# Neighbourhood attention with rows' and context's scores in one two-bank tile, and an output projection that begins with the first pair of heads

## The chip, the core and the metric

The kernel runs on one core of a Trainium2 chip. The metric is the time of one execution on the device, in microseconds (us); smaller is better. Profiles come from one execution each, recorded by the hardware profiler; the engines are TensorE (PE, with its weight loads as PEld), VectorE (DVE), ScalarE (ACT), GpSimd (POOL) and SyncE (SP), which issues the DMAs.

## What is computed

One layer of a diffusion backbone on 1024 latent tokens (16 rows of 64) and 256 context tokens, width 1024. Cut to what matters here:

```python
o_na = neighborhood_attention(q, k, v, k_ctx, v_ctx, rpb)     # 8 heads of 64
o_g, _ = bidirectional_gdn(...)                               # 4 heads of 128, two directions
y = concat([o_na * silu(na_z), o_g * silu(g_z)]) @ w_out
x = x + gate * rmsnorm(y, g_post)
```

Each query of the attention sees a window of 8 rows by 16 columns of latent keys, with a learned bias for each row and column offset, and all 256 context keys, in one softmax:

```python
s_loc = q_r . k_win + bias          # 128 window scores
s_ctx = q_r . k_ctx                 # 256 context scores
p = softmax(concat([s_loc, s_ctx]))
out = p_loc . v_win + p_ctx . v_ctx
```

The gated delta scan runs forwards and backwards over chunks, each step from the state of the one before.

## The kernel before, in words

Phases 0 to 2 (to about 555 us) project the inputs, convolve, and prepare the scan's chunk matrices. This part of the program is the same in both kernels. `phase_b` is the mixed stage: `na_attn` (line 597) and `delta_scan` (line 1170) are generators that yield between pieces of work, and `phase_b` (lines 1460 to 1463) takes pieces of the scan in a fixed proportion to those of the attention. The matmuls of both are chained in the order in which they are written (`pe`, line 592), so PE runs them in that order; the other engines' queues are ordered by the scheduler of the tile framework, and a tile's buffer is given to its next user when all readers of the whole tile are done.

The attention works on 32 units: 4 pairs of heads, 2 halves of the rows (rt), 4 blocks of columns (ct). A unit has two half-units, one for each head of the pair, numbered i. For a half-unit:

- `na_scores` (line 716). POOL adds bias and mask (gm, line 729; not for ct = 2, which takes that of ct = 1). PE makes 256 context scores into the tile pc (line 736) and 288 or 384 window scores into pl (line 739), two matmuls each, since a query is split in a high and a low part. DVE reduces pc to its negated maximum mi (line 744); a second DVE pass over pl and gm writes the negated biased scores and, starting from mi, the negated maximum nm (line 745). ACT takes the exponential of the rows' scores from SBUF (line 746), then that of the context's scores from pc (line 747), each with its own sum.
- `na_turn` (line 751), one iteration later: PE transposes the context's two blocks back into pc (line 754), ACT copies them out (tcx, line 756), PE transposes the rows' three blocks into pl (line 758), DVE copies them out (tl, line 760).
- `na_values` (line 763): matmuls of the values (lines 769 and 774), for both halves of a unit at once, into po.

pc and pl have two buffers each, of one PSUM bank. At the end of a half of the rows, `values` and `end` divide by the sums and multiply by the gate (lines 622 to 639); a finished pair goes to the DRAM buffer m_dram, the last pair is split straight into a high and a low part for the projection (`split_m`, line 704).

A scan step (`delta_step`, line 1194) has three phases for PE (lines 1210, 1228 and 1239, two directions each, two instructions per direction), with POOL (kd line 1204, vb line 1208), DVE (y line 1212, the new state line 1242) and ACT (vn lines 1231 and 1233) between them, and two products for the output (lines 1217 and 1250).

`phase4` (line 1301) multiplies m, in eight blocks k of 128 channels, by w_out: three matmuls of 512 columns for each block and output tile (lines 1337 to 1339). Seven of the first eight output tiles are accumulated block by block in the order `W_ORDER`; block 3, the last pair, comes first. The weights are split into high and low parts in pieces of 512 columns, each loaded to one of two buffers, copied by ACT and subtracted by POOL (`split_piece`, line 693); four blocks and one high part are split early, in buffers that the attention and the scan have given up (`w_out_early`, line 672).

Of the kernel before, what the change touches and what calls it, by code (L numbers as in the profile page):

```python
# [11 lines left out]
F32 = mybir.dt.float32  # L12
# [8 lines left out]
P = 128  # L21
# [115 lines left out]
W_ORDER = [3, 0, 1, 2, 4, 5, 6, 7]  # L137


class K:  # L140
# [456 lines left out]
    def na_attn(self, na, ps):  # L597
# [11 lines left out]

        pairs = {0: load(0)}  # L610
# [4 lines left out]
        def values(j):  # L615
# [17 lines left out]
        def end(j):  # L633
# [12 lines left out]
            if p == 2:  # L646
                self.wait_w = 6
                self.w_out_early(self.pf, [("qh0", 8), ("ql0", 8), ("qh1", 8), ("ql1", 8), ("kk0", 10), ("kk1", 10)])

        for i in range(2 * len(units) + 3):  # L650
            if i < 2 * len(units):
                j, hh = divmod(i, 2)
                p, rt, ct = units[j]
                if (ct, hh) == (0, 0):
                    sums[p, rt] = self.nw.tile([P, 4, 2, 2], F32, name=f"sums{p}_{rt}", tag="sums", bufs=2)
# [12 lines left out]
            self.split_piece()  # L668
# [3 lines left out]
    def w_out_early(self, pool, tags):  # L672
        for tag, n in tags:
            w = pool.tile([P, n, P], F32, name=f"wo_{tag}{len(self.wos)}", tag=tag, bufs=1 if pool is self.pf else 2).rearrange(
                "p t c -> p (t c)")
            for o in range(0, n * P - D + 1, D):
                self.wos.append(w[:, o:o + D])
                if len(self.wos) % 2 == 0:
                    self.split_w(W_ORDER[len(self.wos) // 2 - 1], *self.wos[-2:])

    def split_w(self, k, hi, lo):
        self.wo[k] = (hi.bitcast(F32R), lo.bitcast(F32R))
        self.pieces.extend((k, o, hi[:, o:o + 512], lo[:, o:o + 512]) for o in (0, 512))
        self.load_pieces()

    def load_pieces(self):
        while self.pieces and len(self.staged) < 2:
            k, o, hi, lo = self.pieces.pop(0)
            raw = self.g3.tile([P, 512], F32, name=f"wor{k}_{o}", tag="wor", bufs=2)
            self.load(raw, self.I["w_out"][k * P:(k + 1) * P, o:o + 512], self.na_last)  # L690
            self.staged.append((raw, hi, lo))

    def split_piece(self, n=1):
        nc = self.nc
        if self.wait_w:
            self.wait_w -= 1
            return
        for _ in range(min(n, len(self.staged) + len(self.pieces))):
            raw, hi, lo = self.staged.pop(0)
# [814 lines left out]
```

## Time and profile before

| | us |
|---|---|
| median of 3 runs | 890.77 |
| the three runs | 889.36, 890.77, 899.58 |
| the profiled execution | 898.68 |
| its span, first to last instruction | 896.9 |
| first scores matmul of the attention (line 736) | 555.6 |
| first matmul of the output projection (line 1337) | 797.7 |
| PE busy | 837.1 |
| DVE, ACT, POOL busy | 542.1, 416.9, 352.8 |

The profiled execution is 7.9 us above the median; sums are made against its own time. In the rows of the profile, a group stands with its count, its busy time, the mean of one instruction in ns, and behind the second bar the engine's idle time just before it with what ended that idle time. In the rows by stretch stand the stretch, its length, then busy time with the number of instructions for PE, PEld, DVE, ACT and POOL, the granted clock of PE (1.00 is full), the busy share of the DMA engines and GB/s. In the timeline stand start, length, engine, line and operation. In a chain of waits stand start, length and what ran.

### The profile page before, as it was taken

To read this page: it belongs to the slowest core of one execution; us is meant where nothing else is said; L and a number is where in the kernel's file an instruction comes from. 1 tells how busy PE (TensorE), PEld (TensorE's weight loads), DVE (VectorE), ACT (ScalarE), POOL (GpSimd) and SP (SyncE) were. 2 spreads that over 40 slices of the span, in tenths; PEclk is the share of its full clock that TensorE was granted. 3 is DMA by queue.
4 is the path that set the end of the run, shared out by engine and by line. 5 is a ranking of instruction groups with operands and counts; after the bars stand their busy time and mean duration, and the time that the engine had idled before them with its cause. 6 is when DMAs were issued, how large, how long until landed. Compare 5 with 4: busy or idle time off the path is not lost.

```text
span 896.9 us, 16578 instructions
## 1 busy us (share of the span) xinstructions
PE 837.1 (93%) x6082; PEld 704.4 (79%) x6082; DVE 542.1 (60%) x1179; ACT 416.9 (46%) x1165; POOL 352.8 (39%) x415
## 2 busy tenths in 40 slices
PE   6999999999999979898989997899899999989996
PEld 4678887888788858688877876788788888868885
DVE  3453454556536699779649433577677787781332
ACT  4253535745653554563143533556455555661210
POOL 1333221734453442345512112646546566643110
PEclk9899999999999999999998986799999999989999
DMA  9687442265365535743899857978829523251251
GB/s 339 248 284 253 131 127 85 83 217 169 106 200 174 151 100 176 196 107 93 299 259 253 214 189 288 347 169 217 301 77 294 160 80 133 71 193 66 96 183 51
DMA packets 95175, 160.97 MB, mean 179 GB/s; under 512 B 28581, under 2 KB 55542, under 8 KB 92918
## 3 DMA queue, kind: packets, MB, share of 16 engines
q1 hardware_dynamic: 87606, 146.25, 52.5%
q10 hardware_dynamic: 7488, 13.67, 4.9%
q8 instruction: 48, 0.79, 0.4%
q14 instruction: 33, 0.27, 0.1%
HBM read 110.82 MB, written 52.42 MB: 182 GB/s over the span
## 4 chain that ended last, share of the span: by engine, by line
PE 61%; DVE 19%; DMA 11%; ACT 3%; issue 3%; SPq 2%; POOL 1%; DVEq 0%; POOLq 0%; ACTq 0%
PE py L1337 3%; PE py L1339 3%; PE py L1338 3%; DVE tb L1063 3%; DVE vb L1066 3%; PE pz L461 2%; PE pz L465 2%; PE pz L466 2%; DMA pm_dram<-pm 2%; PE pl L739 2%; PE po L774 2%; PE po L769 2%; PE pa L1228 2%; PE pc L736 2%; DMA tm_dram<-tm 2%
## 5 line engine op out<-in xcount | busy, mean ns | idle before, releaser
L729 POOL TENSOR_TENSOR gm<-gt,mk 128x288 f32<-128x288 f32 (+1 forms) x48 | 46.3, 969 | 40.4 <-DVE nm L745 40.4
L1204 POOL TENSOR_SCALAR kd<-kt,kd 128x128 f32<-128x128 f32 x72 | 42.7, 604 | 28.0 <-PE pa L1239 27.9
L746 ACT ACTIVATE pt<-pt,nm 128x288 f32<-128x288 f32 (+1 forms) x64 | 36.7, 574 | 30.2 <-DVE nm L745 29.9
L760 DVE COPY tl<-pl 96x384 f32<-96x384 f32 (+1 forms) x64 | 35.3, 552 | 17.3 <-PE pl L758 16.4
L745 DVE CUSTOM_DVE_ANT_0 pt<-pl,gm,mi 128x288 f32<-128x288 f32 (+1 forms) x64 | 36.3, 567 | 11.0 <-POOL gm L729 4.7
L1005 ACT ACTIVATE em<-em,gc 128x128 f32<-128x128 f32 x80 | 25.6, 391 | 34.3 <-DMA em<-gc_dram 29.3
L465 PE MATMUL pz<-hl,wh_gz 128*128 128x512 f32 x96 | 39.9, 415 | 0.0
L466 PE MATMUL pz<-hh,wl_gz 128*128 128x512 f32 x96 | 39.5, 412 | 0.0
L461 PE MATMUL pz<-hh,wh_gz 128*128 128x512 f32 x96 | 39.4, 410 | 0.0
L474 PE MATMUL pv<-wh_nv,hh 128*128 128x264 f32 x128 | 35.7, 298 | 2.0 <-ACT hh L263 1.6
L1208 POOL TENSOR_SCALAR vb<-v,beta 128x128 f32<-128x128 f32 x40 | 24.2, 606 | 32.6 <-DVE y L1212 16.7
L475 PE MATMUL pv<-wh_nv,hl 128*128 128x264 f32 x128 | 36.9, 293 | 0.0
L476 PE MATMUL pv<-wl_nv,hh 128*128 128x264 f32 x128 | 35.9, 290 | 1.0 <-DVE wl_nv L447 1.0
L1391 ACT ACTIVATE finv<-py 128x512 f32<-128x512 f32 x16 | 9.6, 599 | 57.3 <-PE py L1339 39.1
L1063 DVE TENSOR_TENSOR tb<-ab,vb 120x31 f32<-120x31 f32 (+15 forms) x62 | 30.2, 487 | 9.9 <-DMA ab<-ab_dram 8.3
L872 DVE SCALAR_TENSOR_TENSOR acc_v<-xp_v,cols,acc_v 128x1282 f32<-128x1282 f32 x16 | 29.1, 1818 | 10.9 <-ACT acc_v L870 10.6
L1392 DVE TENSOR_TENSOR finv<-py,ggb 128x512 f32<-128x512 f32 x16 | 11.0, 690 | 40.6 <-ACT finv L1391 40.5
L744 DVE TENSOR_REDUCE mi<-pc 128x1 f32<-128x256 f32 x64 | 26.9, 420 | 12.4 <-PE pc L736 11.6
L1024 POOL TENSOR_SCALAR_AFFINE_SELECT qe<-qe 128x256 f32<-128x256 f32 x32 | 24.2, 759 | 24.7 <-DVE qe L1023 24.3
L758 PE MATMUL pl<-c,pt 128*96 128x128 f32 (+1 forms) x192 | 32.1, 277 | 0.0
L1020 DVE SCALAR_TENSOR_TENSOR pm<-pk,beta,em 128x128 f32<-128x128 f32 x80 | 23.6, 343 | 13.1 <-PE pk L1013 10.9
L872 DVE SCALAR_TENSOR_TENSOR acc_q<-xp_q,cols,acc_q 128x1024 f32<-128x1024 f32 x16 | 20.5, 1284 | 17.0 <-ACT acc_q L870 16.7
(433 smaller groups left out, 2907.5 us busy)
## 6 DMA issues: line engine op xcount, KB each, us to landing
wada<-in_w_ada SPq DMA_DIRECT2D x16, 512.0 KB, 6.9
em<-gc_dram SPq DMA_DIRECT2D x20, 256.0 KB, 4.1
pm_dram<-pm SPq DMA_DIRECT2D x20, 256.0 KB, 3.2
pmf<-pm_dram SPq DMA_DIRECT2D x8, 640.0 KB, 7.0
tm_dram<-tm SPq DMA_DIRECT2D x8, 640.0 KB, 7.5
kk<-qk_dram SPq DMA_DIRECT2D x16, 320.0 KB, 9.1
tm<-tm_dram SPq DMA_DIRECT2D x4, 1280.0 KB, 16.1
kq_dram<-kq SPq DMA_DIRECT2D x4, 1152.0 KB
```

The costliest lines, as they stand in the source:

```text
L461: r = nc.tensor.matmul(ps, wh, xh, start=(k == 0), stop=False)
L465: nc.tensor.matmul(ps, wh, xl, start=False, stop=False)
L466: nc.tensor.matmul(ps, wl, xh, start=False, stop=(k == KC - 1))
L474: nc.tensor.matmul(ps, xh, wh, start=(k == 0), stop=False)
L475: nc.tensor.matmul(ps, xl, wh, start=False, stop=False)
L476: nc.tensor.matmul(ps, xh, wl, start=False, stop=(k == KC - 1))
L729: nc.gpsimd.tensor_tensor(self.gm[hh][:, :n].rearrange("p (n c r) -> p n c r", c=nco, r=4), gv, self.mk[:, mo:mo + n].rearrange("p (n c r) ...
L745: nc.vector.tensor_tensor_reduce(pt[:, :n], pl[:, :n], gm[:, :n], -1.0, mi, ALU.add, ALU.min, nm)
L746: nc.scalar.activation(pt[:, :n], pt[:, :n], AF.Exp, bias=nm, scale=-1.0, accum_out=sums[:, ct, hh, 0:1])
L872: nc.vector.scalar_tensor_tensor(av, xp[:, s0 + tap:s0 + tap + 1282 - s0], wc(tap), av, ALU.mult, ALU.add)
L1063: nc.vector.tensor_tensor(t3, bc(ab[:, 0:m, m:m + 1], [r, m, n]), bc(vb[:, m:m + 1, m:], [r, m, n]), ALU.mult)
L1204: nc.gpsimd.tensor_scalar(kd[d], kt_[:, t, :], self.kd[:, h, d, t:t + 1], None, ALU.mult)
```

## The change

- **One tile for a half-unit's scores.** sc has two banks: the rows' scores end at column 512 (pl), the context's lie from 512 to 768 (pc). gm becomes one of three fixed tiles of 640 columns whose last 256 are set to zero once; the bias and mask end at column 384. One DVE pass over 544 or 640 columns takes the place of the reduce and the pass, one exponential with one sum that of the two; the sums tile loses a dimension, and with it one addition for each half of the rows.
- **The turn.** All five transposes are written first, then the two copies. tcx, tl and the scan's y have one buffer less.
- **The start.** The scan begins two yields later and then runs slightly denser; its first kd and vb are ordered behind the last gm that was written before them.
- **The projection.** Block 0 comes first and block 3 second. After pair 2 the weights of blocks 0 and 3 are split early, and m of block 0 is read back from m_dram and split with the same pieces (ACT and POOL); block 1's weights follow in the last head of the scan, and half of block 2's. Pieces are split one per half-unit, two half-units or more after their load. The two-bank tiles serve as two output tiles each.

The core of the diff:

```diff
-W_ORDER = [3, 0, 1, 2, 4, 5, 6, 7]
+W_ORDER = [0, 3, 1, 2, 4, 5, 6, 7]
...
+        self.gms, self.gmi = [self.nw.tile([P, 640], F32, name=f"gm{i}") for i in range(3)], 0
+        for g in self.gms:
+            nc.gpsimd.memset(g[:, 384:], 0.0)
...
-            v = sums[p, rt]
-            nc.vector.tensor_tensor(rs.rearrange("p (a b) -> p a b", a=4), v[:, :, :, 0], v[:, :, :, 1], ALU.add)
-            nc.vector.tensor_scalar(rs, rs, 2.0, None, ALU.mult)
+            nc.vector.tensor_scalar(rs, sums[p, rt].rearrange("p a b -> p (a b)"), 2.0, None, ALU.mult)
...
             if p == 2:
-                self.wait_w = 6
-                self.w_out_early(self.pf, [("qh0", 8), ("ql0", 8), ("qh1", 8), ("ql1", 8), ("kk0", 10), ("kk1", 10)])
+                self.clock += 4
+                w = [self.pf.tile([P, n], F32, name=f"early_{t}", tag=t)[:, :D]
+                     for t, n in (("qh0", S), ("ql0", S), ("qh1", S), ("ql1", S), ("kk0", S + CT), ("kk1", S + CT))]
+                self.split_w(W_ORDER[0], *w[:2])
+                self.split_w(W_ORDER[1], *w[2:4])
+                self.ms[0] = tuple(v.bitcast(F32R) for v in w[4:])
+                self.split_later(self.m_dram[0:P, :], *w[4:])
+                self.clock -= 4
...
-            self.split_piece()
+            self.split_piece(1, 2)
...
         if ct != 2:
-            self.gm[hh] = self.nw.tile([P, 384], F32, name=f"gm{p}_{u}_{hh}", tag="gm", bufs=3)
-            nc.gpsimd.tensor_tensor(self.gm[hh][:, :n].rearrange("p (n c r) -> p n c r", c=nco, r=4), gv,
+            self.gm[hh] = self.gms[self.gmi % 3]
+            self.gmi += 1
+            r = nc.gpsimd.tensor_tensor(self.gm[hh][:, 384 - n:384].rearrange("p (n c r) -> p n c r", c=nco, r=4), gv,
                                     self.mk[:, mo:mo + n].rearrange("p (n c r) -> p n c r", c=nco, r=4), ALU.add)
+            self.last_gm = r.ins.name
...
-        pc = ps.tile([P, 512], F32, name=f"pc{p}_{u}_{hh}", tag="sc", bufs=2)[:, :256]
-        pl = ps.tile([P, 512], F32, name=f"pl{p}_{u}_{hh}", tag="sl", bufs=2)
+        sc = ps.tile([P, 1024], F32, name=f"sc{p}_{u}_{hh}", tag="sc", bufs=2)
+        pl, pc = sc[:, :512], sc[:, 512:768]
...
-        nc.vector.tensor_reduce(mi, pc, AX.X, ALU.max, negate=True)
-        nc.vector.tensor_tensor_reduce(pt[:, :n], pl[:, :n], gm[:, :n], -1.0, mi, ALU.add, ALU.min, nm)
-        nc.scalar.activation(pt[:, :n], pt[:, :n], AF.Exp, bias=nm, scale=-1.0, accum_out=sums[:, ct, hh, 0:1])
-        self.last_exp = nc.scalar.activation(pt[:, 384:640], pc, AF.Exp, bias=nm,
-                                             accum_out=sums[:, ct, hh, 1:2]).ins.name
+        nc.vector.tensor_tensor_reduce(pt[:, 384 - n:], sc[:, 512 - n:768], gm[:, 384 - n:], -1.0, 3.0e38, ALU.add, ALU.min, nm)
+        self.last_exp = nc.scalar.activation(pt[:, 384 - n:], pt[:, 384 - n:], AF.Exp, bias=nm, scale=-1.0,
+                                             accum_out=sums[:, ct, hh:hh + 1]).ins.name
...
+        for rc in range(3):
+            self.pe(nc.tensor.transpose(pl[:m, (rc + 1) * P:(rc + 2) * P], pt[:, 384 + (rc - 3) * m:384 + (rc - 2) * m], self.ident))
+        tcx = self.nw.tile([P, 2, P], F32, name=f"tcx{nm}", tag="tcx", bufs=3)
         nc.scalar.copy(tcx.rearrange("p c q -> p (c q)"), pc)
...
+                    w = [g3.tile([P, n, P], F32, name=f"early_{t}", tag=t, bufs=2).rearrange("p t c -> p (t c)")
+                         for t, n in (("o", 8), ("tm", 20))]
+                    self.spare = w[1][:, D:2 * D]
+                    self.split_w(W_ORDER[2], w[0], w[1][:, :D])
...
+                if (h, i) == (0, 0):
+                    self.order(r, self.last_gm)
...
-        late[W_ORDER[4]] = (self.wos[8], tl("wl", W_ORDER[4]))
+        late[W_ORDER[3]] = (self.spare, tl("wl", W_ORDER[3]))
+        late[W_ORDER[4]] = (tl("wh", W_ORDER[4]), tl("wl", W_ORDER[4]))
...
-        tags = [tag for tag, n in banks.items() for _ in range(n)]
+        tags = ["sc", "sc", "sc", "sc", "po", "pa0", "pa1", "os"]
...
-                    while done < min(118, (i + 1) * 118 // 130):
+                    while done < min(118, 1 + max(0, i - 2) * 117 // 127):
```

How the instructions move, at three places. First POOL, at the start of the mixed stage (vb and kd are the scan's, gm the attention's). Before:

```order
L1208 TENSOR_SCALAR vb_1_1_5774<-v_5737,beta 128x128
L1208 TENSOR_SCALAR vb_1_0_5819<-v_5737,beta 128x128
L1208 TENSOR_SCALAR vb_1_9_5887<-v_5737,beta 128x128
L1204 TENSOR_SCALAR kd_0_0_5770<-kt_5738,kd 128x128
L1204 TENSOR_SCALAR kd_1_1_5772<-kt_5738,kd 128x128
L1204 TENSOR_SCALAR kd_0_1_5812<-kt_5738,kd 128x128
L729 TENSOR_TENSOR gm_0_0_5721<-gt_0_5284,mk 128x288
L729 TENSOR_TENSOR gm_0_1_5751<-gt_1_5286,mk 128x288
```

Changed:

```order
L612 MEMSET gm_5718 128x256
L612 MEMSET gm_5719 128x256
L612 MEMSET gm_5720 128x256
L732 TENSOR_TENSOR gm_5718<-gt_0_5284,mk 128x288
L732 TENSOR_TENSOR gm_5719<-gt_1_5286,mk 128x288
L732 TENSOR_TENSOR gm_5720<-gt_0_5284,mk 128x384
L1209 TENSOR_SCALAR kd_0_0_5785<-kt_5739,kd 128x128
L1209 TENSOR_SCALAR kd_1_1_5787<-kt_5739,kd 128x128
L1215 TENSOR_SCALAR vb_1_1_5789<-v_5738,beta 128x128
```

The first three gm moved ahead of all of the scan's work on POOL.

Second DVE, in the last unit of the loop (a name's last numbers are unit and head; y, s and o are the scan's). Before:

```order
L744 TENSOR_REDUCE mi_7_0_8998<-pc_7_0_8992 128x1
L745 ISA pt_7_0_9000,nm_7_0_8999<-pl_7_0_8993,gm_7_0_8990,mi_7_0_8998 128x288
L745 ISA nm_7_0_8999 128x1
L760 COPY tl_6_1_9020<-pl_6_1_8927 128x384
L1242 SCALAR_TENSOR_TENSOR s_0_8_9025<-s_0_7_8950,egl,pa_0_8316 128x128
```

Changed:

```order
L748 ISA pt_7_0_8706,nm_7_0_8705<-sc_7_0_8700,gm_5719 128x544
L748 ISA nm_7_0_8705 128x1
L1251 SCALAR_TENSOR_TENSOR s_0_8_8727<-s_0_7_8663,egl,pa_0_8078 128x128
L1251 SCALAR_TENSOR_TENSOR s_1_3_8730<-s_1_4_8666,egl,pa_1_8079 128x128
L762 COPY tl_6_1_8724<-sc_6_1_8643 128x384
```

The reduce is gone, the pass is longer, and the copy tl of the half-unit before it stands behind the pass in both, here behind the scan's two new states as well.

Third PE, behind the scan's last step (pos is the scan's output, sc the last turn, py the projection's output tiles). Before:

```order
L1250 MATMUL pos_8485<-vn_0_9_9085,qe_7703 128x128
L1250 MATMUL pos_8485<-vn_1_2_9088,qe_7703 128x128
L754 MATMUL pc_7_1_9042<-c_60,pt_7_1_9050 128x128 x2
L758 MATMUL pl_7_1_9043<-c_60,pt_7_1_9050 96x128 x3
L769 MATMUL po_1_8844<-tcx_7_1_9104,vcx 64x128
```

Changed:

```order
L1259 MATMUL pos_8250<-vn_0_9_8780,qe_7534 128x128
L1346 MATMUL py_1_8866<-early_qh_8151,early_kk_8155 128x512
L1347 MATMUL py_1_8866<-early_qh_8151,early_kk_8156 128x512
L1348 MATMUL py_1_8866<-early_ql_8152,early_kk_8155 128x512
L1259 MATMUL pos_8250<-vn_1_2_8783,qe_7534 128x128
L756 MATMUL sc_7_1_8743<-c_60,pt_7_1_8749 128x128 x2
L758 MATMUL sc_7_1_8743<-c_60,pt_7_1_8749 96x128 x3
L1346 MATMUL py_0_8867<-early_qh_8151,early_kk_8155 128x512
L1347 MATMUL py_0_8867<-early_qh_8151,early_kk_8156 128x512
L1348 MATMUL py_0_8867<-early_ql_8152,early_kk_8155 128x512
L1346 MATMUL py_8863<-early_qh_8151,early_kk_8155 128x512
```

Before, all 21 products of the first block stand behind the values, the transposes prt of the last half of the rows and the first half of the scan's output ot. Now 18 products stand between the scan's last matmul and ot's second half, and the second block (pair 3) follows it.

More of the change, by code (lines that the diff above doesn't have):

```diff
@@ L687, in load_pieces, with split_piece @@
         while self.pieces and len(self.staged) < 2:
[L688 to L693, printed above, removed]
-        nc = self.nc
[L695 to L699, printed above, removed]
+            src, hi, lo = self.pieces.pop(0)
+            self.nraw += 1
+            raw = self.g3.tile([P, 512], F32, name=f"raw{self.nraw}", tag="wor", bufs=2)
+            self.load(raw, src, self.na_last)
+            self.staged.append((self.clock, raw, hi, lo))
+    def split_piece(self, n=1, wait=0):
+        nc = self.nc
+        self.clock += 1
+        for _ in range(n):
+            if not self.staged or self.clock - self.staged[0][0] < wait:
+                return
+            _, raw, hi, lo = self.staged.pop(0)
             self.order(nc.scalar.copy(hi.bitcast(F32R), raw), self.last_exp)
@@ L1355, in phase4 @@
                     next(parts, None)
+                    self.split_piece(2)
+                    if i == 2:
+                        for _ in last:
+                            pass
                     if i == 3:
```

49 lines of the change are left out of this document (20 added, 29 removed).

## The prediction

> **What bounds the kernel now.** The page's first rows come first: TensorE is busy for 93% of the span, every other engine for 60% or less.
>
> ```profile
> span 896.9 us, 16578 instructions
> PE 837.1 (93%) x6082; PEld 704.4 (79%) x6082; DVE 542.1 (60%) x1179; ACT 416.9 (46%) x1165; POOL 352.8 (39%) x415
> ```
>
> So a change of DVE and ACT work pays only where TensorE stands waiting for them, or runs at a low clock because it stood. The diff touches the mixed stage (attention and scan, 555.5 to 790) and its two ends. The busy times by stretch come next; behind the stretch stand its length and PE's busy time, and ahead of the last two numbers the granted clock.
>
> ```profile
> 556.00:560.00 4.00, 2.66 (x12) 2.37 (x11) 1.08 (x3) 0.63 (x2) 2.45 (x5) 0.50 1.00 422
> 560.00:564.00 4.00, 0.33 (x2) 0.33 (x3) 1.05 (x4) 1.47 (x6) 4.00 (x6) 0.50 1.06 376
> 564.00:570.00 6.00, 6.00 (x29) 5.94 (x28) 3.17 (x9) 2.89 (x12) 3.52 (x5) 0.52 0.96 396
> 570.00:580.00 10.00, 9.93 (x98) 8.72 (x97) 7.18 (x23) 5.60 (x19) 4.73 (x7) 1.00 1.03 348
> 640.00:700.00 60.00, 57.00 (x524) 51.25 (x523) 45.83 (x144) 34.83 (x132) 35.13 (x50) 1.00 0.70 201
> 700.00:750.00 50.00, 47.14 (x439) 42.33 (x439) 39.13 (x123) 28.56 (x111) 29.97 (x42) 1.00 0.36 127
> 555.50:790.00 234.50, 217.19 (x1948) 194.63 (x1948) 172.06 (x538) 134.58 (x500) 137.92 (x187) 0.96 0.62 187
> ```
>
> PE is idle for 234.50 - 217.19 = 17.3 us of the stage. The start holds 5.0 of it (1.34 and 3.67 between 556 and 564), with half a clock until 570. The steady loop has little: 5.9 us idle in the 110 us from 640 to 750. Behind the stage there is one more hole:
>
> ```profile
> 793.00:797.00 4.00, 0.66 (x5) 0.46 (x5) 3.09 (x4) 2.32 (x3) 3.84 (x5) 0.75 0.93 334
> 797.00:800.50 3.50, 3.50 (x11) 2.92 (x12) 3.50 (x4) 0.83 (x2) 1.06 (x1) 0.50 0.64 249
> 805.00:889.00 84.00, 84.00 (x364) 67.83 (x363) 26.70 (x41) 16.19 (x38) 13.00 (x19) 1.00 0.32 108
> ```
>
> PE is idle for 3.3 us there, then works 3.5 us at half clock, and from 805 to 889 it does not stop at all: the output projection is PE's own work, and what is gained ahead of it stays gained.
>
> **The start.** The waits between 555 and 600 and the timeline name the hole:
>
> ```profile
> POOL vb L1208 <- DMA v<-vt_dram: 12.4, 1, 12.4
> DVE pt L745 <- POOL gm L729: 4.5, 2, 4.2
> 556.46 0.44 PE L739 MATMUL pl<-kk,ql 128*128 128x288 f32 x1
> 557.37 0.44 PE L739 MATMUL pl<-kk,ql 128*128 128x288 f32 x1
> 561.06 4.70 POOL L729 TENSOR_TENSOR gm<-gt,mk 128x288 f32<-128x288 f32 x5
> 563.67 0.69 PE L754 MATMUL pc<-c,pt 128*128 128x128 f32 x2 [5.01 <-ACT pt L747]
> 570.30 0.66 PE L769 MATMUL po<-tcx,vcx 128*64 128x128 f32 x8
> ```
>
> The scores are done at 557.8, but the first bias sum (gm) stands on POOL behind three vb and three kd, the first of which waits 12.4 us for a DMA; so the first pass on DVE starts late and the first transposes run at 563.67. In the changed order three memsets and three gm stand ahead of every kd and vb, inside POOL's old 12.4 us of waiting, and PE takes the turn of half-unit 0 and the scores of half-unit 2 ahead of the first scan matmul.
>
> Worked from rows: the first pl matmul pair ends at 556.46 + 0.44 = 556.9. The wide pass takes 0.78 and the one exponential 0.75 (both worked out in the next part), with 0.1 between them as in the chain there: transposes from about 558.6 in place of 563.67. Two of them took 0.69 at half clock, so five some 1.4; the copy tl takes 0.55 (its row below); the scores of half-unit 2 start near 560.6, the scan's first matmuls near 561.7, the second turn near 562.5, the second scan phase and the fourth scores after it, and the first values (L769) near 565 instead of 570.30. That is 5.3 us, but PE has then done two scan phases fewer (four matmuls each, 0.44 us a phase at full clock, the last row of the chain below), 0.9 us that comes later: 4.4, and a little for the clock, which should be back some us ahead of 569.75. I take **-4.5**; bounds: -2, if the first turns run into each other's copies, and -6, if the clock comes back at 563.
>
> The clock may come back later than that: from 564 to 570 PE was busy for all six us and the clock was still 0.52. If the new start, half of which are transposes, keeps half a clock 3 us longer than I take it, half of that, 1.5 us, is lost: rival (e). The Trainium skill, TensorE: Matmul & The Clock Gate, Part 4, has a rule that would make it so: transposes do not count as busy for the clock gate. By that rule the sum would be 882.0. The trace does not bear it out where the clock is up: from 640 to 750, with five transposes in every half-unit, it was 1.00 throughout.
>
> **The loop.** Groups by form, and the waits of 640 to 750 at the two buffers:
>
> ```profile
> L744 DVE TENSOR_REDUCE mi<-pc 128x1 f32<-128x256 f32 x64 | 26.9, 420 | 12.4 <-PE pc L736 11.6
> L745 DVE CUSTOM_DVE_ANT_0 pt<-pl,gm,mi 128x288 f32<-128x288 f32 x32 | 16.5, 517 | 7.2 <-POOL gm L729 4.7 <-DVE mi L744 0.7 <-ACT osq L1267 0.7
> L745 DVE CUSTOM_DVE_ANT_0 pt<-pl,gm,mi 128x384 f32<-128x384 f32 x32 | 19.8, 617 | 3.8 <-DVE mi L744 0.9 <-ACT vn L1233 0.7 <-PE pa L1210 0.5
> L760 DVE COPY tl<-pl 128x384 f32<-128x384 f32 x32 | 17.8, 555 | 9.8 <-PE pl L758 9.3
> L746 ACT ACTIVATE pt<-pt,nm 128x288 f32<-128x288 f32 x32 | 17.1, 535 | 12.9 <-DVE nm L745 12.5
> L746 ACT ACTIVATE pt<-pt,nm 128x384 f32<-128x384 f32 x32 | 19.6, 614 | 17.4 <-DVE nm L745 17.4
> L747 ACT ACTIVATE pt<-pc,nm 128x256 f32<-128x256 f32 x64 | 29.2, 457 | 0.0
> PEld pc L736 <- ACT tcx L756: 3.8, 7, 0.9
> PEld pl L739 <- DVE tl L760: 1.9, 6, 0.5
> ```
>
> DVE: the reduce (420 ns) goes; the pass grows by 256 elements. From 517 at 288 and 617 at 384 an element costs 1.04 ns, so 783 and 883 (estimates). A half-unit costs 420 + 517 = 937 before and 783 after, -154 ns, 64 times -9.9 us; the sum of two sums per half (eight instructions) goes as well. ACT: 535 + 457 = 992 becomes one exponential; at 0.82 ns an element (614 - 535 over 96) 745 and 825, so -247 ns, 64 times -15.8 us, and one accumulator read less. None of this is on PE. What it is worth is read from the chain of waits, where such a stretch sets PE's next start:
>
> ```profile
> 693.42 0.42 DVE mi L744
> 693.99 0.62 DVE pt L745
> 694.71 0.71 ACT pt L746 x2
> 695.42 0.45 ACT pt L747 x2
> 695.88 0.38 ACT tcx L756
> 696.30 0.51 PE pc L736 x2
> 696.82 0.53 PE pl L739 x2
> 697.35 0.44 PE pa L1228 x4
> ```
>
> The exponentials stand ahead of tcx in ACT's queue, and tcx frees the pc tile. PE waited for it seven times in 110 us, two of the four pairs of heads: 14 in the stage, at 0.25 each 3.5 us less. The passes waited 0.7 + 0.9 us for mi in all: 1.0 of that. Against it: pc and pl are now one tile, so the first scores matmul of half-unit i+2 waits for the later of two copies, ACT's tcx and DVE's tl, where before only the third matmul waited for tl. Above, the scores started at 696.30 and the pl matmuls waited until 696.82; that 0.5 us now comes first, and about 0.4 of pc work follows where it lay under the wait. The six such waits in 110 us make about 12 in the stage: 12 times 0.2 (between 0 and 0.4) = 2.4. 3.5 + 1.0 - 2.4 = 2.1: net **-2**, bounds -12.3 (all idle time outside the start goes) and +20 (below). Fewer tcx, tl and y buffers: a buffer's reader is one iteration ahead of its next writer on PE, so nothing.
>
> **The end.** The timeline:
>
> ```profile
> 795.16 3.45 DVE L1284 TENSOR_TENSOR o<-o,rq_y_o 128x512 f32<-128x512 f32 x2
> 795.20 1.04 ACT L712 CAST m<-zs 128x1024 fp32r<-128x1024 f32 x1
> 797.73 3.33 PE L1337 MATMUL py<-wo_o,m 128*128 128x512 f32 x7
> 804.67 0.94 PE L1337 MATMUL py<-wo_tm,mh 128*128 128x512 f32 x3
> ```
>
> Before, the first 21 products need pair 3, which is finished last; they run from 797.73 at half clock, and product 22 starts at 804.67. Changed, 18 products of pair 0 stand between the last scan and value matmuls, at 0.23 us each (84.00 us for the 364 of the row 805 to 889), 4.2 us of work for the hole behind 790. Pair 3 itself gets later: DVE now scales o twice (3.45 us from 795.16, to 798.6) ahead of the product zs; with that product (512 elements, some 0.75 at the pass's rate) and ACT's cast (1.04) the high half is there near 800.4. So product 19 starts near 800.4, product 22 would at 801.1, where before it did at 804.67: 3.6, and 0.2 for ot transposes that are already done. **-3.8**; bounds -1.6 (cast two us later) and -5.
>
> What pays for it: one weight pair more is split inside the projection, five instead of four, ten pieces of 512 columns; each set of 21 products lasts 4.9 us and covers two pieces. The split of m for pair 0 moves into the loop, on ACT and POOL, which are idle there for 40% and more (rows 640 and 700). The queue of SP keeps its order up to the second pair; behind it only loads change places that the loop does not wait for.
>
> **The sum.** 4.5 + 2 + 3.8 = 10.3. The profiled execution took 898.68 (its span 896.9 and 1.8 around it), which gives 888.4. It stood 7.9 above the median of the runs, 890.77; the same difference from the median gives **880.5**.
>
> **Rivals.** (a) *The loop closes up.* With 25 us less on DVE and ACT all other waits of PE go: 12.3 us in place of 2, 870.2. For it: DVE is busy for 77% from 640 to 750 and stands on the chain. Against it: most waits there end on DVE's scan work, which stays. (b) *The shared tile rules.* The copy tl stands on DVE behind the next half-unit's pass, now 266 ns longer, and scores wait for it at their first matmul. If that costs the 0.4 us of pc work in 48 of 64 half-units it is 19.2, and 890.8 - 8.3 + 19.2 = 901.7, slower; start and end are used up from 21 half-units on. For it: in the chain above tl came 0.5 us after tcx. Against: only some 12 half-units wait for tl now. (c) *The scan sets the pace.* Its first matmul moves from 557.8, behind the second scores, to about 561.7; if its serial chain of 40 steps decides, the start gains nothing: 885.0. For it: every phase waits for the one before. Against: a chain that set the pace would leave PE more than 5.9 idle us in 110. (d) *The end does not fill.* The products of pair 0 are there, but pieces of the third or fourth weight pair come late, and PE waits in the projection what it saved: 884.3. (e) *The clock comes back late* at the start: 880.5 + 1.5 = 882.0; for and against it stands above.
>
> **Chances.** Forecast 0.45, (a) 0.20, (b) 0.10, (c) 0.10, (d) 0.07, (e) 0.08. The forecast's own range is 874 to 887. For 8 in 10 the range reaches into (a) and half-way to (b), and takes in that single runs lay between 889.36 and 899.58: 866 to 892. A measurement of this kernel tells about 2% from no change, 17.8 us, so faster means under 873.0: most of (a) and the edge of the forecast, 0.20; slower, over 908.6, is (b) at its worst, 0.04; within 2%, 0.76.
>
> **What would show it.** Start: transposes near 559, clock 1.00 by 564 to 566, values near 565. Loop: passes of 783 and 883 ns, exponentials of 745 and 825, PE idle in 110 us of loop near 5. End: 18 products ahead of 800, no clock of 0.50 behind the stage, product 22 near 801. It is wrong if pc matmuls wait for tl in more than 20 half-units, if the loop's unit gets longer than before, or if PE stops between the first and the last product for more than a us.

## The result: slower by 3.4%, and where the time went

The changed kernel takes 924.06 us at the median (4 runs, 922.35 to 924.51). The kernel before, run beside it, has 892.0 (4 runs, 889.36 to 899.58). The ratio is 1.0342, interval 1.0276 to 1.0407: 32.1 us slower, where 880.5 and a range up to 892 were forecast.

The page of the changed kernel, its span and busy times:

```profile
span 922.8 us, 16433 instructions
PE 840.9 (91%) x6082; PEld 703.7 (76%) x6082; DVE 529.2 (57%) x1106; ACT 402.9 (44%) x1038; POOL 354.9 (38%) x420
```

DVE and ACT do 13 and 14 us less than before, as the change meant. TensorE runs the same 6082 matmuls in a span that is 25.9 us longer, and for 22 of them it is idle. The busy times by stretch (stretch, its length, busy times of PE, PEld, DVE, ACT, POOL, then the clock, DMA share and GB/s) say in which stage:

```profile
562.00:564.00 2.00, 1.58 (x19) 1.27 (x20) 1.14 (x3) 0.00 (x0) 0.92 (x2) 0.88 0.99 412
564.00:570.00 6.00, 4.82 (x42) 4.03 (x38) 3.44 (x12) 2.90 (x8) 2.60 (x4) 1.00 1.03 426
640.00:700.00 60.00, 50.88 (x453) 44.72 (x453) 37.25 (x111) 26.57 (x85) 30.82 (x43) 1.00 0.60 169
700.00:750.00 50.00, 42.43 (x380) 36.96 (x379) 31.40 (x94) 22.36 (x70) 23.10 (x33) 1.00 0.27 86
552.40:813.70 261.30, 219.06 (x1904) 191.81 (x1903) 157.95 (x457) 118.22 (x362) 135.38 (x184) 0.97 0.57 169
```

In the 110 us of steady loop PE is idle for 16.7 us, where it was 5.9 before. From the first scores matmul to the start of the last half-unit's scores it takes 261.3 us; before it was 229.9 (555.6 to 785.5). PE's waits there (who, for whom, us in total, times, longest) have one large row:

```profile
PE sc L741 <- DVE tl L762: 38.5, 52, 1.8
```

Before, the same place had:

```profile
PE pc L736 <- ACT tcx L756: 3.7, 8, 0.7
PE pl L739 <- DVE tl L760: 2.0, 7, 0.5
```

The groups by form show that the shorter instructions did come (mean ns behind the bar), and what the two copies waited for:

```profile
L748 DVE CUSTOM_DVE_ANT_0 pt<-sc,gm 128x544 f32<-128x544 f32 x32 | 23.1, 723 | 15.4 <-PE sc L744 10.8 <-POOL vb L1215 3.2 <-POOL rb L632 1.2
L748 DVE CUSTOM_DVE_ANT_0 pt<-sc,gm 128x640 f32<-128x640 f32 x32 | 26.4, 825 | 25.8 <-PE sc L744 23.6 <-POOL gm L732 1.6 <-POOL vb L1215 0.6
L749 ACT ACTIVATE pt<-pt,nm 128x640 f32<-128x640 f32 x32 | 26.5, 828 | 48.7 <-DVE nm L748 48.7
L760 ACT COPY tcx<-sc 128x256 f32<-128x256 f32 x64 | 23.3, 365 | 19.7 <-PE sc L758 19.3
L762 DVE COPY tl<-sc 128x384 f32<-128x384 f32 x32 | 17.7, 552 | 4.5 <-ACT tcx L760 4.4
```

The last two rows are new: tcx, which reads only the context's half, waits for the rows' transposes (L758), and tl waits for **tcx**, an instruction that writes nothing tl reads. In the chain of waits of the changed kernel one turn reads:

```profile
714.11 0.22 PE sc L756 x2
714.33 0.34 PE sc L758 x3
714.69 0.38 ACT tcx L760
715.09 0.56 DVE tl L762
...
715.70 0.50 PE sc L741 x2
```

Transposes, first copy, second copy, next scores: four steps in a row. In the timeline of the kernel before a turn reads:

```profile
709.60 0.38 PE L754 MATMUL pc<-c,pt 128*128 128x128 f32 x2
709.82 0.49 PE L758 MATMUL pl<-c,pt 128*96 128x128 f32 x3
710.08 0.37 ACT L756 COPY tcx<-pc 128x256 f32<-128x256 f32 x1 [0.16 <-PE pc L754]
710.35 0.55 DVE L760 COPY tl<-pl 96x384 f32<-96x384 f32 x1 [0.93 <-PE pl L758]
710.96 0.37 PE L736 MATMUL pc<-kk,qh 128*128 128x256 f32 x1
```

There tcx starts ahead of the last transpose's end, and tl beside it. Over all 64 half-units of the two traces, tl starts 0.04 us (median) behind the last transpose in the kernel before and 0.60 behind it in the changed one. That is tcx (0.37), a hand-over from ACT to DVE (0.12) and the short wait ahead of tcx. The semaphores in the traces say the same: in the kernel before all 64 copies tl wait for a semaphore that PE raises, in the changed kernel all 64 wait for the one that ACT raises, and none starts ahead of tcx's end. Why one tile brings this wait with it is not shown here; that it does, is.

**Theory**: pc and pl as halves of one tile make the copy tl wait for the copy tcx, so that a half-unit's transposes, two copies and the next scores stand in series; this is the loss, and start and end were gains. **Rivals**: the single long pass and exponential; the order of the loop and the scan's new place; fewer buffers; the wait of the first scores matmul alone, without the series.

### The profile page after: what moved, and what is told of

It reads as the page before. It is cut to its first block, busy times and chain, and to the rows that moved or that the text cites. A ratio compares the mean times of both kernels' runs of the same rounds, so it can differ in the third digit from the quotient of the medians.

```text
span 922.8 us, 16433 instructions
## 1 busy us (share of the span) xinstructions
PE 840.9 (91%) x6082; PEld 703.7 (76%) x6082; DVE 529.2 (57%) x1106; ACT 402.9 (44%) x1038; POOL 354.9 (38%) x420
## 4 chain that ended last, share of the span: by engine, by line
PE 62%; DVE 18%; DMA 9%; ACT 4%; issue 4%; SPq 2%; POOL 1%; DVEq 0%; POOLq 0%; ACTq 0%
PE py L1346 3%; PE py L1347 3%; PE py L1348 3%; DVE tl L762 3%; PE sc L741 3%; DVE tb L1065 3%; DVE vb L1068 2%; PE pz L465 2%; PE pz L466 2%; PE pz L461 2%; DMA pm_dram<-pm 2%; PE po L776 2%; PE sc L744 2%; PE po L771 2%; PE pa L1237 2%
## 5 line engine op out<-in xcount | busy, mean ns | idle before, releaser
L749 ACT ACTIVATE pt<-pt,nm 128x544 f32<-128x544 f32 (+1 forms) x64 | 50.5, 789 | 78.7 <-DVE nm L748 78.1
L748 DVE CUSTOM_DVE_ANT_0 pt<-sc,gm 128x544 f32<-128x544 f32 (+1 forms) x64 | 49.5, 774 | 41.2 <-PE sc L744 34.4
L741 PE MATMUL sc<-kk,qh 128*128 128x256 f32 x64 | 25.0, 390 | 38.6 <-DVE tl L762 38.5
L741 PEld LDWEIGHTS sc<-kk,qh 128*128 128x128 f32 x64 | 12.3, 192 | 49.9 <-DVE tl L762 49.8
L762 DVE COPY tl<-sc 96x384 f32<-96x384 f32 (+1 forms) x64 | 35.2, 550 | 10.5 <-ACT tcx L760 10.2
L1408 DVE TENSOR_TENSOR finv<-py,ggb 128x512 f32<-128x512 f32 x16 | 10.9, 689 | 48.5 <-ACT finv L1407 48.5
L466 PE MATMUL pz<-hh,wl_gz 128*128 128x512 f32 x96 | 38.6, 402 | 0.0
L1251 DVE SCALAR_TENSOR_TENSOR s<-s,egl,pa 128x128 f32<-128x128 f32 x64 | 20.6, 343 | 29.3 <-PE pa L1248 29.3
L1065 DVE TENSOR_TENSOR tb<-ab,vb 120x31 f32<-120x31 f32 (+15 forms) x62 | 32.3, 521 | 8.7 <-DMA ab<-ab_dram 7.1
```

The costliest lines, as they stand in the source:

```text
L466: nc.tensor.matmul(ps, wl, xh, start=False, stop=(k == KC - 1))
L741: self.pe(nc.tensor.matmul(pc, a[:, u * P:(u + 1) * P], kk[:, S:S + CT], start=(i == 0), stop=(i == 1)))
L748: nc.vector.tensor_tensor_reduce(pt[:, 384 - n:], sc[:, 512 - n:768], gm[:, 384 - n:], -1.0, 3.0e38, ALU.add, ALU.min, nm)
L749: self.last_exp = nc.scalar.activation(pt[:, 384 - n:], pt[:, 384 - n:], AF.Exp, bias=nm, scale=-1.0, accum_out=sums[:, ct, hh:hh + 1]).in ...
L762: nc.vector.tensor_copy(tl[:m, :], pl[:m, P:])
L1065: nc.vector.tensor_tensor(t3, bc(ab[:, 0:m, m:m + 1], [r, m, n]), bc(vb[:, m:m + 1, m:], [r, m, n]), ALU.mult)
```

## The experiments

Each time is the median of its runs, each difference against the kernel before on the same chip.

### Two tiles again

```
-        sc = ps.tile([P, 1024], F32, name=f"sc{p}_{u}_{hh}", tag="sc", bufs=2)
-        pl, pc = sc[:, :512], sc[:, 512:768]
+        pc = ps.tile([P, 512], F32, name=f"pc{p}_{u}_{hh}", tag="sc", bufs=2)[:, :256]
+        pl = ps.tile([P, 512], F32, name=f"pl{p}_{u}_{hh}", tag="sl", bufs=2)
...
+        nc.vector.tensor_reduce(mi, pc, AX.X, ALU.max, negate=True)
```

> The changed kernel with pc and pl as two one-bank tiles again, and so with the reduce mi, two exponentials, the copy tcx between the transposes, and the sum of two sums; its start (bias sums ahead of kd and vb, memsets, the scan two half-units later), its end and its buffers stay. Theory (one tile puts transposes, tcx, tl and the next scores in series): everything that was lost is gone and the gains of start and end stay, some 4 and 2 us against the kernel before (892): 884 to 889; waits of scores for tl at their first matmul gone. Rival (the other order of the loop, the later start of the scan or the fewer buffers cost it): 905 or more, as these all stay.

Measured: 902.22, 10.4 above the kernel before (891.8). The waits for tl at the first scores matmul are gone and 22 us with them, but the time is not the expected 884 to 889, and is just under the rival's 905. The waits name a new one:

```profile
PE pos L1264 <- DMA qe<-qe_dram: 8.2, 2, 4.4
```

It has a second cost, the clock behind the stop (the number ahead of the last two):

```profile
628.00:632.00 4.00, 0.53 (x2) 0.53 (x3) 0.00 (x0) 0.00 (x0) 0.00 (x0) 0.63 1.07 319
632.00:636.00 4.00, 4.00 (x21) 4.00 (x20) 2.31 (x8) 1.76 (x6) 1.06 (x2) 0.52 0.75 274
636.00:640.00 4.00, 4.00 (x45) 3.66 (x45) 2.15 (x9) 2.31 (x10) 2.27 (x4) 1.00 0.78 243
```

After 4.4 us of standing, PE works 4 us at half clock. The Trainium skill, TensorE: Matmul & The Clock Gate, Part 1 (What's actually happening), gives an idle window of about 3.4 us as what halves the clock; these rows agree. But a shorter stop was enough elsewhere: in the changed kernel PE stood for 1.80 us from 767.36, and its clock was 0.50 from 771 to 774. Where the two differ the measurement decides, so a stop of this length can cost clock too. In SP's queue qe has another place. Here, at the second head:

```profile
611.12 0.33 SPq L154 DMA_DIRECT2D v<-vt_dram  x1
612.22 0.32 SPq L154 DMA_DIRECT2D tm<-tm_dram  x1
613.72 0.32 SPq L154 DMA_DIRECT2D kq<-kq_dram  x1
614.88 0.32 SPq L154 DMA_DIRECT2D vv<-v_dram  x1
615.90 0.32 SPq L154 DMA_DIRECT2D qe<-qe_dram  x1
```

and in the kernel before:

```profile
620.20 0.33 SPq L154 DMA_DIRECT2D tm<-tm_dram  x1
621.37 0.32 SPq L154 DMA_DIRECT2D qe<-qe_dram  x1
622.63 0.32 SPq L154 DMA_DIRECT2D v<-vt_dram  x1
```

The scan's later steps (the line with 117 // 127) moved qe, the load that PE then waits for, behind four others.

### The shared tile alone

```
# on the kernel before
+        sc = ps.tile([P, 1024], F32, name=f"sc{p}_{u}_{hh}", tag="sc", bufs=2)
+        pl, pc = sc[:, :512], sc[:, 512:768]
# and the three transposes of the rows ahead of tcx
```

> The kernel before with one change: pc and pl are halves of one two-bank tile (and so five transposes and then the copies). Two passes, two exponentials, start, end and buffers as before. Theory (the tile): 33 us or more above the kernel before, 920 to 932, with waits of the first scores matmul for tl of 30 us or more and tl waiting for tcx. Rival (the wide pass and the wide exponential, as longer single steps between scores and transposes, cost it): within 5 us of the kernel before, 887 to 897.

Measured: 926.33, 34.5 above the kernel before. Two passes, two exponentials, the old start and end, and the whole loss is there (the waits for tl, 28.9 us, are a little under the 30 that were expected). Its largest wait, and the group of tl:

```profile
PE sc L736 <- DVE tl L760: 28.9, 50, 1.5
```

```profile
L760 DVE COPY tl<-sc 128x384 f32<-128x384 f32 x32 | 17.7, 553 | 3.9 <-ACT tcx L758 3.9
```

So the rival of the long pass and exponential falls. Two things came along with the tile in this run: the three transposes are written ahead of tcx, and the projection's output tiles share the two-bank tiles. The second cost nothing to be seen (from the last scores matmul to the last product 103.7 us, before 103.3); no run has the first with two tiles. The Trainium skill, PSUM — Partial Sum Buffer (PSUM bank collisions raise a hardware error), wants engines kept apart by bank and group of 32 partitions, and says that accesses to different banks run clean. The two halves lie in different banks, so by that rule the copies could have run side by side, as they do with two tiles (tcx at 710.08 and tl at 710.35 above); the rows show that with one tile they do not.

### The loop's part alone

```
# on the kernel before: one tile, one pass, one exponential, transposes then copies,
# three gm of 640 columns, tcx and tl in 3 buffers, y in 2
```

> The kernel before with the loop's part of the change alone: one tile, one pass, one exponential, transposes and then copies, three bias buffers of 640 columns, buffers 3, 3 and 2; start, scan schedule and end as before. Theory (the tile costs it, start and end were gains): the changed kernel plus the 4 to 6 us of start and end, 927 to 931. Rival (the new schedule of scan and projection costs a good part of it): clearly under the changed kernel, 900 to 915. Rival (the merging of pass and exponential gains what the forecast said, about 5 us): 5 under the kernel with the shared tile alone.

Measured: 925.86, 34.1 above, a little under the expected 927 to 931. Beside the run above, merging pass and exponential (14 us less on DVE, 16 on ACT), together with the fewer buffers, is worth 0.5 us, far inside the uncertainty. In both kernels PE waits only once for an exponential (5.0 and 5.7 us, at the start); what it waits for lies behind the transposes, where nothing was made shorter.

### Only the wait of the first scores matmul

```
# on the kernel before
-        for i, a in enumerate(qs): ... matmul(pc, ...)
         for i, a in enumerate(qs): ... matmul(pl, ...)
+        for i, a in enumerate(qs): ... matmul(pc, ...)
```

> The kernel before, two tiles, with one change: the two pl matmuls stand ahead of the two pc matmuls, so that the first scores matmul waits for tl, as in the changed kernel, but tl does not wait for tcx. This is the wait that the prediction counted. By its price (12 waits of 0.2 us, and mi some 0.25 us later behind the last matmul): 892 to 896. If that wait alone makes the loss: 915 or more, with 25 us or more of waits of pl for tl. Theory (the larger part is that one tile puts tcx and tl in series, 365 and 550 ns): between, 895 to 905, with 6 to 15 us of waits for tl.

Measured: 894.81, 2.5 above (ratio 1.0017, 0.9991 to 1.0044). The waits for tl, where 5.7 us stood before for tl and tcx together:

```profile
PE pl L737 <- DVE tl L760: 10.9, 23, 1.3
```

The price that the prediction set on this wait, 2.4, fits the 2.5, though with 23 waits in place of its 12, so the agreement of the sum is partly luck. This wait is not what made the loss.

### One copy on ACT, and both copies on DVE

```
# on the changed kernel: one copy in place of two
+        tl = self.nw.tile([P, 640], F32, name=f"tl{nm}", tag="tl", bufs=3)
+        nc.scalar.copy(tl, sc[:, P:768])
```

> The changed kernel with one copy of all 640 turned columns on ACT in place of tcx on ACT and tl on DVE (the rows' transposes 128 columns wide, so that all that is copied has been written). Theory (two copies in series behind the transposes): the series gets shorter by tl's 550 ns and a wait and longer by 384 columns on ACT, some 0.31 us at 0.82 ns each: about 0.3 us in each of 52 half-units, 15 us: 906 to 914, with waits of the scores for the copy of some 23 us in place of 38. Rival (wide pass and exponential): ACT does more, so 924 or above.

```
# on the changed kernel: tcx on DVE
-        nc.scalar.copy(tcx.rearrange("p c q -> p (c q)"), pc)
+        nc.vector.tensor_copy(tcx.rearrange("p c q -> p (c q)"), pc)
```

> The changed kernel with tcx copied by DVE too, directly ahead of tl: still two copies in series behind all five transposes, but on one engine. DVE gets 64 copies of about 420 ns more (27 us), ACT 365 ns each less. Theory (the length of the series counts, not whose engine it is): the series stays 0.95 to 1.0 us long: 920 to 930. Rival (the hand-over from ACT to DVE is the cost): 0.1 us or more less in each of 52 half-units, 5 to 10 us faster: 914 to 919.

Measured: 913.82 with one copy (22.0 above the kernel before) and 914.77 with both on DVE (22.5 above), each some 10 us better than the changed kernel. With one copy, its group and the waits of PE:

```profile
L760 ACT COPY tl<-sc 128x640 f32<-128x640 f32 x64 | 43.8, 685 | 23.4 <-PE sc L758 23.2
```

```profile
PE sc L741 <- ACT tl L760: 20.2, 32, 3.0
PE pos L1257 <- DMA qe<-qe_dram: 6.9, 2, 4.2
```

One copy of 685 ns ends 0.73 us behind the last transpose (median), the two in series 1.15. That is 0.42 in each of 52 half-units, 22 us; half of it came, and the qe wait, which the slower loop had hidden, is back. With both on DVE, one turn in the timeline:

```profile
705.15 0.49 PE L758 MATMUL sc<-c,pt 128*128 128x128 f32 x3
705.74 0.41 DVE L760 COPY tcx<-sc 128x256 f32<-128x256 f32 x1
706.07 0.55 DVE L762 COPY tl<-sc 128x384 f32<-128x384 f32 x1
706.76 0.36 PE L741 MATMUL sc<-kk,qh 128*128 128x256 f32 x1 [0.68 <-DVE tl L762]
```

tl starts ahead of tcx's recorded end (by 0.08 us at the median), where across engines it starts 0.12 behind it. The series ends at 0.98 in place of 1.15; 0.17 times 52 is 9.0 us, and 9.6 were measured. The rival in the expectation is right here (914 to 919, where the theory said 920 to 930): the hand-over between engines is part of the price.

### Two tiles, and the scan in its old place

```
# on the kernel with two tiles
-                    while done < min(118, 1 + max(0, i - 2) * 117 // 127):
+                    while done < min(118, (1 + max(0, i - 2) * 117 // 127) if i < 8 else (i + 1) * 118 // 130):
# the second kernel
+                    while done < min(118, (i + 1) * 118 // 130):
```

> The changed kernel with two one-bank tiles, as in the first experiment, and with the scan's steps placed as in the kernel before from the eighth turn of the loop on (the late start of the scan stays for the first eight). In the first experiment the scan matmuls waited 8.2 us for the loads of qe at the second and third head, which its SP queue issues behind v, tm, kq and a part of vv; in this kernel they stand behind tm alone again. Theory (the later scan moved the qe load behind other loads, and the faster loop then waits for it, 8.2 us and a half clock behind it): that wait is under 2 us, and the time is 884 to 891, 11 to 18 under the first experiment and under the kernel before by the 4 and 2 us of start and end at most. Rival (the loads are late because the DMA engines are full, whatever their order): still 6 us or more of waits for qe, 898 to 903.

> As the kernel beside it, but with the scan's steps placed as in the kernel before from the first turn on: of the change stay the bias sums ahead of kd and vb, the projection's order and the buffers. Theory (the start gains by the later scan): 1 to 4 us slower than the kernel beside it, 886 to 893, first values later. Rival (the start gains by POOL's order alone): the same as the kernel beside it within 1 us.

Measured: 893.28 and 891.06, 1.0 above and 1.2 under the kernel before (ratios 1.0011, 0.9982 to 1.0039, and 0.9989, 0.9959 to 1.0019). The qe waits fall to 1.1 and 0.5 us, with qe again ahead of v, kq and vv in SP's queue: the scan's place caused them, most likely by the order of the loads, which no run changes alone. The first lies above its expected 884 to 891, and the second, expected to be 1 to 4 us slower than the first, is not: the later scan at the start shows no gain. But neither kernel has the gains of start and end, and a wait of the second names why, with ACT's timeline:

```profile
PE pa L1253 <- ACT vn L1245: 3.1, 2, 2.9
```

```profile
738.04 0.62 ACT L704 CAST early_o<-raw 128x512 fp32r<-128x512 f32 x1 [5.38 <-DMA raw<-in_w_out]
738.56 0.36 ACT L1245 ACTIVATE vn<-pa,beta 128x128 f32<-128x128 f32 x1
```

The first piece of the early weight pair stands in ACT's queue before its data is there, and the scan's vn and an exponential stand behind it.

### The start alone, and two tiles with the piece later

```
# on the kernel before: gm remembers its name, the first kd and vb are ordered behind it
+            self.last_gm = r.ins.name
...
+                if (h, i) == (0, 0):
+                    self.order(r, self.last_gm)
```

> The kernel before with the start's part alone: the first kd and vb wait on POOL for the last bias sum issued so far. Nothing else of the change. Theory (the start is a gain of its own): first transposes some 4 us earlier, 3 to 4.5 us less, 887.5 to 889. Rival (the scan or a DMA sets the pace of the first 15 us or gives it back by the end of the loop): the same as the kernel before, 891 to 893.

```
# on the kernel with two tiles and the old scan
+                    self.clock += 2
                     self.split_w(W_ORDER[2], w[0], w[1][:, :D])
+                    self.clock -= 2
```

> Two one-bank tiles, the scan placed as in the kernel before, start and end of the change, and one thing more: the first piece of the early weight pair is put on ACT two half-units later. In the run without that (891.1 us), ACT stood 5.4 us for the DMA of this piece, and vn and so TensorE 2.9 us behind it, with less clock after it. Theory (start and end are worth the 3.5 and 4.1 us that the trace shows, and this stall took them back): the stall goes, 3 to 5 us less, 886 to 888, the fastest of all. Rival (the loop or the projection gives it back elsewhere): 890 to 893, as the kernel before.

Measured: 886.65 for the start alone, 4.6 under the kernel before (ratio 0.9961, 0.9939 to 0.9982), and 885.47 for two tiles with the start, the end and the later piece, 5.8 under it (0.9931, 0.9908 to 0.9955). This one beats both kernels. Its largest waits in the stage are the old ones:

```profile
PE pc L743 <- ACT tcx L763: 4.2, 9, 0.7
PE pa L1255 <- POOL kd L1216: 2.4, 3, 0.8
PE pl L746 <- DVE tl L767: 2.0, 7, 0.5
```

### One tile, with what else was found mended

```
# on the kernel with one copy on ACT, and on the changed kernel with its two copies
+                    while done < min(118, (i + 1) * 118 // 130):
...
+                    self.clock += 2
                     self.split_w(W_ORDER[2], w[0], w[1][:, :D])
+                    self.clock -= 2
```

> The changed kernel with its one tile, one pass and one exponential, one copy of 640 columns on ACT in place of the two copies, the scan placed as in the kernel before, and the later first piece. The earlier run with one copy (913.8) also waited 6.9 us for qe, with half a clock behind it. Theory (the series behind the transposes is 0.14 us longer than with two tiles at the median, 0.25 at the mean, in some 50 half-units): 7 to 13 us above the kernel with two tiles, 895 to 903. Rival (with the series short, the 25 us less of work on DVE and ACT pay): under 891.

> The changed kernel, its one tile and two copies kept, with the scan placed as in the kernel before and the later first piece. Theory (in the changed kernel the series of copies slows the loop so far that the moved loads and the piece are hidden): 919 to 926, as the changed kernel, with 35 us or more of waits for tl. Rival (they cost the changed kernel as well): 908 to 916.

Measured: 899.12 with one copy (7.8 above the kernel before), 914.68 with two copies (23.4 above). The first is in its expected range and 13.6 over the kernel with two tiles and mended alike, so with one tile the merging did not pay even with the shortest series that was run. The second answers to the rival, not to the theory: 8.7 of the changed kernel's 32.1 us go with the scan's place and the early piece. Two more runs, the changed kernel with one of the two mendings each:

> The changed kernel with the later first piece alone (its scan stays where the change puts it). Together with the scan of before this gave 914.7, 9.4 us less than the changed kernel. If the piece is what costs (ACT stood 3.3 us for its DMA in the changed kernel too): 916 to 919. If the scan's place is: 922 to 925, unchanged.

> The changed kernel with the scan placed as in the kernel before alone. If the scan's place costs the 9 us: 914 to 918. If the piece does: 921 to 924.

Measured: 921.12 with the later piece (2.8 better than the changed kernel, each against its own kernel before) and 917.24 with the scan in its old place (6.7 better). The first is inside the uncertainty: its runs, 917.91 to 922.99, overlap those of the changed kernel. The second is not: its highest run, 919.62, lies under the lowest of the changed kernel, 922.35. So it is mostly the scan's place, and not through qe, for which the changed kernel did not wait. The group of the first scores matmul in the second run, beside the 38.6 us of the changed kernel:

```profile
L741 PE MATMUL sc<-kk,qh 128*128 128x256 f32 x64 | 25.0, 390 | 31.1 <-DVE tl L762 30.5
```

Between a half-unit's last transpose and the scores that wait for its copies, the old place puts 8 or 12 other matmuls in 40 of 62 half-units and 4 in 17; the new one 8 or 12 in 34 and 4 in 23 (counted in the traces). So with the new place less work lay over the same series. That this is the cause is argued from the counts; it fits the 8.0 us less of waits for tl.

## Why the prediction was wrong

The steps from kernel to kernel are: start alone -4.6; two tiles with start, end and the later piece -5.8, so end and fewer buffers -1.2 (between two intervals of some 2 us each way, so zero is not excluded); the one tile with its merged pass (23.4 against -5.8, all else alike) **+29.2**; the scan's place and the early piece together **+8.7**. Their sum is the measured 32.1 by construction; what the runs show is the size of each step.

**The start, -4.5: right in kind; the size is partly luck.** The run of the start alone has only the new order on POOL and gained 4.6 (1.6 to 5.4 by its interval). The forecast's working also had the later scan, which gained nothing with two tiles. In the changed kernel's timeline:

```profile
552.38 0.58 PE L741 MATMUL sc<-kk,qh 128*128 128x256 f32 x1
555.48 0.69 PE L756 MATMUL sc<-c,pt 128*128 128x128 f32 x2 [0.91 <-ACT pt L749]
563.27 0.66 PE L771 MATMUL po<-tcx,vcx 128*64 128x128 f32 x8
```

The transposes run 3.1 us behind the first scores, as forecast (558.6 against 555.5), the values 10.9 behind them (9.5 forecast, 14.7 before), and the clock is 0.88 from 562 and 1.00 from 564. Rival (e) did not come: nearly half of PE's work from 555.5 to 562 was transposes, and the clock was back on time.

**The loop, -2, measured +34.1 by itself: the step that failed is "the first scores matmul of half-unit i+2 waits for the later of two copies".** It took the copies as independent, with their starts as before, and priced only that the wait comes first: 12 waits of 0.2 us. That part alone is worth 2.5 us, as run by itself. What the step left out is that one tile also orders its readers: tl starts 0.56 us later at the median, and PE has 52 waits of 0.74 us in place of 15 of 0.38. (The counts of waits in the working were those of the weight loads, PEld, in 110 us; PE's own were 8 for tcx and 7 for tl in the whole stage.) Rival (b) had the direction and too small a size (48 half-units of 0.4, 19.2 us), from another cause, tl behind the next pass on DVE; it got a chance of 0.10. The gains in this step, 3.5 for tcx and 1.0 for mi, are not there either with one tile: 0.5 in all, inside the uncertainty. The passes take 723 and 825 ns (783 and 883 forecast), the exponentials 749 and 828 (745 and 825); those sizes were near enough, and worth nothing off the path.

**"Behind it only loads change places that the loop does not wait for": no harm in the changed kernel, but wrong where the loop is faster.** With a loop that is not held up by the series, PE waits 8.2 us for qe. And the moved scan steps were priced for the start alone; in the loop, by the counts above, they are the cover under which a turn's copies run.

**The splits in the loop "on ACT and POOL, which are idle there": wrong in one place.** The prediction says it of m; the piece that cost was one of w_out. With two tiles and the old scan, its cast of 0.62 stood 5.38 us in ACT's queue for its data, and PE 2.9 us behind it. In the changed kernel the same mending gained 2.8 us, inside the uncertainty.

**The end, -3.8: right in kind, its size open.** The 18 products stand where they were put. From the end of the last scores matmul to the end of the last product it takes 101.4 us in the changed kernel and 99.2 in the best one, where it takes 103.3 before and 101.9 with the start alone, whose end is the old one. So the traces give the best kernel 2.7 to 4.1 us, the runs only the 1.2 above; the best kernel's stage is 2.7 us longer than that of the start alone (227.2 against 224.5, first to last scores matmul), and no run tells whether the end's work in the loop or the fewer buffers make it so. The half clock behind the old end's hole, on which part of the forecast rests, is not in every execution either: it is in four of the five traces with the old end, and not in that of the start alone. PE did stop for more than a us between products, for the high half of pair 3:

```profile
818.36 0.48 PE L1346 MATMUL py<-early_qh,early_kk 128*128 128x512 f32 x1
828.47 0.59 PE L1346 MATMUL py<-early_qh,early_kk 128*128 128x512 f32 x1 [1.64 <-DVE zs L640]
```

Of the conditions named in advance for being wrong, all three occurred: more than 20 half-units that wait for tl, a longer loop, and this stop. **Fewer buffers, nothing**: no run kept the start and end and undid the buffers, so that is only bounded, by the -1.2 that they share with the end and the 0.5 that they share with the merging.

## What to carry to other kernels

Before two things become halves of one tile, list who reads each half, on which engine: readers that ran side by side may now run one behind the other, and the price is the length of the first plus a hand-over, in every turn in which nothing covers it. Work taken off engines that are not on the path was worth nothing here; look instead at what lies between PE's last write of a buffer and its next one, and at how much other work the schedule puts there. A step that moves a stage's work in program order also moves its loads in the queue and the casts behind them, and a loop that is slow for another reason hides what that costs.

## What the runs showed of the hardware

A copy on DVE that waits for a copy on ACT started 0.12 us behind its end (median of 64 in the changed kernel; 0.06 with the loop's part alone), one behind another on DVE 0.08 us ahead of its recorded end. A stop of PE of 4.4 us was followed by 4 us at a clock of 0.52. A stop of 1.80 us in the changed kernel was followed by 0.50 from 771 to 774, while one of 2.56 us with the start alone (from 781.1) left the clock at 1.00, so in these runs the length of a stop does not decide alone. A copy of 640 columns on ACT took 685 ns, less than 256 on ACT and 384 on DVE together (365 and 550).
